# Convolution inputs and two gates of a hybrid layer as one run of Strassen pairs, with the gates and the residual kept in DRAM

## The chip, the core and the metric

The kernel runs on one core of a Trainium2 chip. The metric is the device time of one execution in microseconds (us). Five engines work side by side, each through its own list of instructions in order: TensorE (PE) multiplies, VectorE (DVE) and ScalarE (ACT) do elementwise work, GpSimd (POOL) does some of it and issues DMAs that add to what lies in SBUF, and SyncE (SP) issues the other DMAs. PE has two clock levels, 2.4 and 1.2 GHz; the profile gives the granted share of full speed.

## The reference

The input is a sequence of 512 positions with 1024 features (float32). Two hybrid layers run one after the other, then a second block that the change does not touch. One hybrid layer, cut to what matters here:

```python
def hybrid_layer(x, positions, ...):
    h = rmsnorm(x, norm_mix)
    proj = h @ w_in
    cb, cc, cu, q, k, v, g, ga, gb = jnp.split(proj, split_points, axis=-1)
    y_conv = short_conv_mixer(cb, cc, cu, conv_w, w_conv_out)   # (cb * conv3(cc * cu)) @ w_conv_out
    y_ret = retention_mixer(q, k, v, g, positions, ret_norm, w_ret_out)
    merged = jax.nn.sigmoid(ga) * y_conv + jax.nn.sigmoid(gb) * y_ret
    x = x + merged @ w_o
    h2 = rmsnorm(x, norm_mlp)
    return x + jnp.square(jax.nn.relu(h2 @ w_up)) @ w_down
```

The convolution inputs cb, cc, cu and the gates ga, gb are 1024 columns each, so five of the products here are 1024 x 1024.

## The kernel before

Activations lie transposed: a tile has 128 features on the partitions and 512 positions, and x is 8 such tiles. To keep float32 accuracy every operand is split into a high and a low part, and each block product is three matmuls (`mm3`, L282 to L284: high x whi, low x whi, high x wlo).

**Weights** come in units of up to eight 128 x 128 blocks, in the order in which PE uses them. SP loads a unit into one of seven raw buffers (`load_to`, L203), so the load of unit u+7 waits until unit u is split. ACT makes the high part (`whi`, L232) and DVE the low part (`wlo`, L233) in `part_to`. Strassen units also need sums of weight blocks: POOL issues a DMA that adds a second stretch of DRAM to the raw buffer (`sum_to`, L214, tile `wa`), and DVE adds one raw unit onto another (L229). `advance` asks for loads 9 units ahead, sums 7 ahead and splits 2 ahead.

**Products.** `dense` makes one 128 x 512 output tile from 8 block products, that is 24 matmuls of 512 columns. `strassen` makes pairs of output tiles with seven half-width products per block pair: 7 x 4 x 3 = 84 matmuls of 256 columns in place of 48 of 512 columns. It takes its operands from seven "factors" of each pair of input tiles, which `halves` makes. Before, only w_up uses it, in four quarters of four pairs. Product f of pair j is written (f, j); PE takes them in an order written out by hand.

**Order of a layer.** In `b1_layer`: the convolution inputs by `dense` for m = 0 to 7 (columns 1024 `ev_c`, 2048 `ev_u`, 0 `ev_b` of w_in); gate ga; w_conv_out (`ev_co`); four retention heads; gate gb; the gate g; w_ret_out (`ev_ro`); w_o; then the MLP. The norm of x is not waited for: its factor `rbc` is multiplied in when a product is taken out of PSUM, and the sum of squares, its reduction by PE (L516) and the broadcast (L528) run beside the first products. Small pieces of work (the norm chain, the rotary tables, retention pieces) lie in a list `bg`; `pulse` takes one off when PE has been given 4.5 us of products (`due`) since the last.

## Time and profile before

| | |
|---|---|
| time, median of 3 runs | 2538.9 us (2536.22 to 2543.73) |
| the profiled execution | 2541.95 us |
| its span in the profile | 2540.2 us |
| PE busy | 2505.2 us (99%), 13150 matmuls |
| DVE, ACT, POOL busy | 1538.8 (61%), 1013.8 (40%), 355.8 (14%) us |
| mean granted PE clock | 0.993 of full |

The span is the stretch that the profile covers; the time has 1.75 us more around it. The profiled execution lies 3.05 us (0.12%) above the median of the three runs.

### The profile page before, as it was taken

The numbers are of one execution on the slowest core, as the hardware profiler recorded it, in microseconds if no ns is written. First come the engines' busy times: TensorE is split into PE (matmuls) and PEld (weight loads), VectorE is DVE, ScalarE is ACT, GpSimd is POOL, SyncE is SP. The second block draws the span as 40 slices with busy tenths as digits, with TensorE's granted clock in tenths as the row PEclk, the third lists the DMA queues.
The fourth block names the chain that finished last, engine by engine and source line by source line (L and its number), as shares of the span: only waits on it lengthen the run. The fifth ranks groups of instructions, "written<-read, shape, count | busy, mean of one in ns | idle before, by whom it ended". The sixth has DMA issues, their size and how long they took to land. (4 is left out here: it accounts for less than half of the span.)

```text
span 2540.2 us, 33110 instructions
## 1 busy us (share of the span) xinstructions
PE 2505.2 (99%) x13150; PEld 2139.2 (84%) x13150; DVE 1538.8 (61%) x2254; ACT 1013.8 (40%) x1672; POOL 355.8 (14%) x338
## 2 busy tenths in 40 slices
PE   8999999999999999999999999999999999999998
PEld 7888988888899888889887998898867888888886
DVE  6544655575666654356467665676679565673773
ACT  4222434353453422234335553354586444322221
POOL 2100110220001211011012101013100111220111
PEclk9999999999999999999999999999999999999999
DMA  5333222265666332322223665563301322233221
GB/s 201 108 98 98 78 75 84 89 176 159 169 191 176 119 100 98 99 86 79 80 96 93 195 190 151 161 187 104 107 27 34 100 92 83 91 100 100 91 95 46
DMA packets 87692, 286.22 MB, mean 113 GB/s; under 512 B 9904, under 2 KB 9904, under 8 KB 87408
## 3 DMA queue, kind: packets, MB, share of 16 engines
q1 hardware_dynamic: 76032, 256.56, 30.5%
q0 software_dynamic: 10784, 26.48, 6.2%
q8 instruction: 103, 1.69, 0.3%
q10 hardware_dynamic: 720, 1.05, 0.1%
q14 instruction: 53, 0.43, 0.1%
HBM read 281.96 MB, written 2.10 MB: 112 GB/s over the span
## 5 line engine op out<-in xcount | busy, mean ns | idle before, releaser
L282 PE MATMUL mm<-hi,whi 128*128 128x512 f32 x2528 | 989.7, 391 | 6.2 <-ACT hi L274 6.2
L284 PE MATMUL mm<-hi,wlo 128*128 128x512 f32 x2528 | 986.3, 390 | 0.1
L283 PE MATMUL mm<-lo,whi 128*128 128x512 f32 x2528 | 985.5, 390 | 0.5 <-DVE lo L277 0.5
L233 DVE TENSOR_TENSOR wlo<-raw,whi 128x1024 fp32r<-128x1024 f32 (+2 forms) x512 | 608.4, 1194 | 288.3 <-ACT whi L232 285.9
L232 ACT ACTIVATE whi<-raw 128x1024 fp32r<-128x1024 f32 (+2 forms) x512 | 502.2, 995 | 373.6 <-PE mm L283 312.3
L284 PEld LDWEIGHTS mm<-hi,wlo 128*128 128x128 f32 x2528 | 475.4, 188 | 103.3 <-DVE wlo L233 3.6
L282 PEld LDWEIGHTS mm<-hi,whi 128*128 128x128 f32 x2528 | 475.9, 188 | 102.6 <-ACT hi L274 6.2
L283 PEld LDWEIGHTS mm<-lo,whi 128*128 128x128 f32 x2528 | 475.8, 188 | 97.8 <-DVE lo L277 1.0
L539 POOL TENSOR_TENSOR ssq<-ssq,sq 128x512 f32<-128x512 f32 x65 | 91.4, 1406 | 537.1 <-ACT sq L274 528.0
L282 PE MATMUL sa<-tf,whi 128*128 128x256 f32 x512 | 147.1, 287 | 5.3 <-ACT y L274 5.3
L284 PE MATMUL sa<-tf,wlo 128*128 128x256 f32 x512 | 147.0, 287 | 1.1 <-DVE wlo L233 1.1
L283 PE MATMUL sa<-tf,whi 128*128 128x256 f32 x512 | 146.1, 285 | 0.0
L214 POOL DMA_DIRECT2D raw<-wa x72 | 62.2, 864 | 504.0 <-DMA raw<-ws 229.1
L769 DVE TENSOR_TENSOR dn<-mm,rbc 128x512 f32<-128x512 f32 x64 | 44.2, 690 | 126.2 <-PE mm L284 126.1
L282 PEld LDWEIGHTS sa<-tf,whi 128*128 128x128 f32 x512 | 99.1, 194 | 6.4 <-ACT y L274 5.7
L284 PE MATMUL sb<-tf,wlo 128*128 128x256 f32 x352 | 99.8, 283 | 1.9 <-DVE wlo L233 1.9
L284 PEld LDWEIGHTS sa<-tf,wlo 128*128 128x128 f32 x512 | 99.2, 194 | 2.6 <-DVE wlo L233 2.5
L283 PE MATMUL sb<-tf,whi 128*128 128x256 f32 x352 | 99.8, 283 | 0.9 <-DVE tf L277 0.9
L282 PE MATMUL sb<-tf,whi 128*128 128x256 f32 x352 | 100.0, 284 | 0.0
L283 PEld LDWEIGHTS sa<-tf,whi 128*128 128x128 f32 x512 | 99.3, 194 | 0.3
L881 PE MATMUL nat<-whi,hi 128*128 128x256 f32 (+2 forms) x320 | 94.9, 297 | 0.0
L882 PE MATMUL nat<-wlo,hi 128*128 128x256 f32 (+2 forms) x320 | 94.2, 294 | 0.0
(361 smaller groups left out, 3170.6 us busy)
## 6 DMA issues: line engine op xcount, KB each, us to landing
raw<-ws SPq DMA_DIRECT2D x444, 512.0 KB, 3.4
raw<-ws SPq DMA_DIRECT2D x64, 256.0 KB, 3.3
raw<-wa POOLq DMA_DIRECT2D x48, 256.0 KB, 5.2
raw<-wa POOLq DMA_DIRECT2D x24, 512.0 KB, 5.5
x<-x SPq DMA_DIRECT2D x8, 256.0 KB, 5.8
raw<-ws SPq DMA_DIRECT2D x4, 384.0 KB, 3.0
dec<-dec SPq DMA_DIRECT2D x1, 1024.0 KB, 10.0
mem<-mem POOLq DMA_DIRECT2D x4, 256.0 KB, 4.9
```

The costliest lines, as they stand in the source:

```text
L214: self.nc.gpsimd.dma_start(self.raw[u][:, at:at + n], self.d["wa"][self.more_at[u]][:, :n], accum_op=ALU.add)
L232: self.nc.scalar.activation(hi[:, :n], w, AF.Copy)
L233: tt(lo[:, :n], w, hi[:, :n].bitcast(F32), op=ALU.subtract)
L282: mm(out, w[0], x[0], start=start, stop=False, **kw)
L283: mm(out, w[0], x[1], start=False, stop=False, **kw)
L284: mm(out, w[1], x[0], start=False, stop=stop, **kw)
L539: self.nc.gpsimd.tensor_tensor(st["ssq"], st["ssq"], q, op=ALU.add)
L769: tt(t, p, self.rbc2, op=ALU.mult)
L881: mm(p, xc[0], w[0][:, :n], start=k == 0, stop=False)
L882: mm(p, xc[0], w[1][:, :n], start=False, stop=False)
```

## The change

In each hybrid layer the convolution inputs of m = 2 to 7 (9 pairs) and both gates (8 pairs) become one run of 17 Strassen pairs; m = 0 and 1 stay dense. The run's factors are made by the new `factors` from x and the split tiles that exist already: four pairs of input tiles, each with nine DVE operations of up to 256 columns and five ACT operations. They stand in `bg` behind the norm chain and the rotary tables, and whatever is still in `bg` after the two dense groups is put out at once, before the first pair. The gates (as sigmoids), the gated convolution m1 and the residual x no longer wait in SBUF: `away` writes each tile of 256 KB to DRAM on ACT's queue, and `back` reads it on SP's queue, ga in `ev_co`, and gb, m1 and x in `ev_ro`. Two additions or products go from POOL to DVE, one scaling from DVE to ACT. The retention heads take background work every 3 us. The first quarter of w_up starts with five products without their last input pair (`early`). The core of the diff:

```diff
+    def away(self, x, what):
+        t = self.dp.tile([P, S], F32, tag=what, name=self.name(what), bufs=KD)
+        self.nc.scalar.dma_start(t, x)
+        return t
+    def back(self, t, what):
+        x = self.slot(what=what)
+        self.nc.sync.dma_start(x, t)
+        return x
...
-            for v in [v for v in w if v < u - 1 and v != self.cur]:
+            for v in [v for v in w if v < min(u - 1, self.pinned) and v != self.cur]:
...
+    def factors(self, xs, k, x1, x2, g1, g2):
+        tt = self.nc.vector.tensor_tensor
+        st, out = {}, {}
+        for f, (m, e) in {1: (k, 0), 2: (k + 1, 0), 3: (k + 1, 1)}.items():
+            out[f] = [t[:, e * H:(e + 1) * H] for t in xs[m]]
+        def split(f, v):
+            t = self.slot(S, True, "tf")
+            out[f] = t[:, :H], t[:, H:]
+            self.act(t[:, :H], v)
+            self.lo(t[:, H:], v, t[:, :H])
+        def first():
+            y, t, n = self.slot(what="ty"), self.slot(what="tu"), self.sm(1, "ng")
+            st["y"], st["t"] = y, t
+            self.nc.vector.tensor_scalar(n, g2, -1.0, None, op0=ALU.mult)
+            self.act(y, x1, AF.Copy, scale=g1)
+            tt(t[:, H:], y[:, :H], y[:, H:], op=ALU.subtract)
+            self.stt(t[:, :H], x2[:, H:], n, y[:, H:])
+            split(5, t[:, H:])
+        def second():
+            y, t, u = st.pop("y"), st.pop("t"), self.slot(what="tv")
+            tt(u[:, :H], t[:, :H], y[:, :H], op=ALU.subtract)
+            self.stt(u[:, H:], x2[:, :H], g2, u[:, :H])
+            for f, v in ((7, t[:, :H]), (6, u[:, :H]), (4, u[:, H:])):
+                split(f, v)
+        return out, [first, second]
...
+        if early:
+            open_pair(1)
+            y0 = unit([(6, 0)], x0)
+            self.pinned = at[1, 0][0]
+            first = [(1, 0), (2, 0), (7, 0), (1, 1), (2, 1)]
+            for x in first:
+                product(*x, ks=range(K - 1), split=1)
+            for f, j in first:
+                product(f, j, ks=[K - 1], split=1)
+                if f == 1:
+                    keep(j, 1)
+                elif f == 2 and j == 0:
+                    self.pinned = x0
+                    self.part_to(y0 + 1)
+                elif f == 7:
+                    self.pinned = MOST
+                    self.part_to(y0 + 2)
...
+        X = []
+        for k in range(0, KD, 2):
+            def begin(k=k):
+                out, steps = self.factors(xs, k, self.x[k], self.x[k + 1], *[self.prm(f"mix{i}", m) for m in (k, k + 1)])
+                X.append(out)
+                self.bg[:0] = steps
+            self.bg.append(begin)
...
-            nc.vector.tensor_scalar(y, z[:, 2:], self.prm(f"conv{i}_2", m), None, op0=ALU.mult)
+            self.act(y, z[:, 2:], AF.Copy, scale=self.prm(f"conv{i}_2", m))
...
-            t, y = self.slot(what="b"), tmp["y"]
-            tt(t, p, self.rbc, op=ALU.mult)
-            nc.gpsimd.tensor_tensor(t, t, y, op=ALU.mult)
-            bz[m] = yield from self.split_late(t)
-        for m in range(KD):
+            y = tmp.pop(("y", m))
+            tt(y, y, self.rbc, op=ALU.mult)
+            tt(y, p, y, op=ALU.mult)
+            bz[m] = yield from self.split_late(y)
+        for m in range(2):
...
-        m1 = [None] * KD
-        def ev_gate(m, p):
-            t = self.slot(what="gate")
-            tt(t, p, self.rbc, op=ALU.mult)
-            self.act(t, t, AF.Sigmoid)
-            m1[m] = t
-        self.dense(xs, [c8(W, 6144, m) for m in range(KD)], ev_gate)
+        while self.bg:
+            self.tick(0.0)
+        for m in range(KD):
+            self.x[m] = self.later[m]
...
+        def gate(what):
+            def ev(m, y):
+                tt(y, y, self.rbc, op=ALU.mult)
+                yield
+                self.act(y, y, AF.Sigmoid)
+                away[what, m] = self.away(y, what)
+            return ev
...
+        evs, pairs = [], []
+        for m in range(2, KD, 2):
+            for o, ev in ((1024, ev_c), (2048, ev_u), (0, ev_b)):
+                evs.append((ev, m))
+                pairs.append([c8(W, o, m), c8(W, o, m + 1)])
...
+        for o, what in ((6144, "ga"), (7168, "gb")):
+            for m in range(0, KD, 2):
+                evs.append((gate(what), m))
+                pairs.append([c8(W, o, m), c8(W, o, m + 1)])
...
+        self.strassen(X, pairs, done)
...
+            t = self.back(away.pop(("ga", m)), "ga")
+            tt(t, p, t, op=ALU.mult)
+            yield
+            away["m1", m] = self.away(t, "m1")
...
+        self.due = 3.0
...
-        sgb = [None] * KD
-        def ev_sgb(m, p):
-            t = self.slot(what="sgb")
-            tt(t, p, self.rbc, op=ALU.mult)
-            self.act(t, t, AF.Sigmoid)
-            sgb[m] = t
-        self.dense(xs, [c8(W, 7168, m) for m in range(KD)], ev_sgb)
...
-            t = self.slot(what="mg")
-            tt(t, p, sgb[m], op=ALU.mult)
-            nc.gpsimd.tensor_tensor(t, t, m1[m], op=ALU.add)
+            t, m1 = self.back(away.pop(("gb", m)), "gb"), self.back(away.pop(("m1", m)), "m1")
+            tt(t, p, t, op=ALU.mult)
+            tt(t, t, m1, op=ALU.add)
+            del m1
+            self.x[m] = self.back(x[m], "x")
...
-            self.strassen(xm, [[c8(f"w_up{i}", (quarter * Q + 2 * j + e) * P, 0) for e in range(2)] for j in range(Q // 2)], up)
+            self.strassen(xm, [[c8(f"w_up{i}", (quarter * Q + 2 * j + e) * P, 0) for e in range(2)] for j in range(Q // 2)], up, quarter == 0)
...
+        if later:
+            self.later[m] = self.away(x, "x")
...
-        self.bg += [scores((0, 1)), scores((2, 3)), lambda: None, outs, var, scale]
+        gap = lambda: None
+        self.bg += [scores((0, 1)), scores((2, 3)), gap, gap, outs, var, scale]
```

What this does to the order on the engines is shown at three places; names end in the buffer number of each program, which is not the same in both.

**POOL at the start of the program.** `ssq` collects the squares of x (`sq`), `rstd` is the norm's factor, `raw7` the eighth unit of weights. Before:

```order
L1787 UNCONDITIONAL_BRANCH [waits barrier_Pool_Activation_PE_DVE_SP_gather]
L539 ISA
L539 TENSOR_TENSOR ssq_30_191<-ssq_30_191,sq_31_193 128x512 [waits Activation_49]
...
L539 TENSOR_TENSOR ssq_30_191<-ssq_30_191,sq_37_241 128x512 [waits Activation_49,Pool_49]
L521 TENSOR_TENSOR rstd_40_282<-ms_39_280,mhalf_100 128x4 [waits DVE_49]
```

and now:

```order
L1906 UNCONDITIONAL_BRANCH [waits barrier_Pool_Activation_PE_DVE_SP_gather]
L226 DMA raw7_161<-wa 128x512 [waits DMAHW4_49,DMAHW1_49,DVE_49]
L624 ISA
L624 TENSOR_TENSOR ssq_30_194<-ssq_30_194,sq_31_196 128x512 [waits Activation_49]
...
L624 TENSOR_TENSOR ssq_30_194<-ssq_30_194,sq_37_244 128x512 [waits Activation_49,Pool_49]
L606 TENSOR_TENSOR rstd_40_285<-ms_39_283,mhalf_102 128x4 [waits DVE_49]
```

The adding DMA of unit 7 stands ahead of the seven additions, and it waits for the load of raw7.

**DVE in the first layer, behind the last product of m = 1** (`b` and `y` are taken from PSUM there, L662 and L755). `turns` and `rest` are the rotary tables' range reduction, `ng`, `tu`, `tv` and `tf` belong to the factors, `wlo8` is the low part of the ninth unit. Before:

```order
L662 TENSOR_TENSOR b_57_414<-mm_56_382,rbc_43_320 128x512
L588 TENSOR_SCALAR turns_60_419<-ang_55_379 128x512
...
L596 TENSOR_SCALAR rest_61_420<-rest_61_420 128x512
L233 TENSOR_TENSOR wlo8_442<-raw8_161,whi8_441 128x1024
L647 TENSOR_TENSOR c_63_461<-mm_62_429,rbc2_44_322 128x512
```

and now:

```order
L755 TENSOR_TENSOR y_53_379<-mm_55_386,y_53_379 128x512
L673 TENSOR_SCALAR turns_58_423<-ang_54_383 128x512
...
L681 TENSOR_SCALAR rest_61_435<-rest_61_435 128x512
L299 TENSOR_TENSOR lo_57_422<-y_53_379,hi_56_421 128x512
L712 TENSOR_TENSOR trig_10_107<-trig_10_107,rbc_43_324 128x512
L713 TENSOR_TENSOR trig_10_107<-trig_10_107,rbc_43_324 128x512
L417 TENSOR_SCALAR ng_64_450<-par_71 128x1
...
L299 TENSOR_TENSOR tf_91_527<-tu_87_515,tf_91_527 128x256
L299 TENSOR_TENSOR tf_93_533<-tv_90_524,tf_93_533 128x256
L245 TENSOR_TENSOR wlo8_543<-raw8_163,whi8_542 128x512
```

Before, one table's reduction (8 operations) lies between this product and wlo8; now both tables' reductions (15), a split, the tables' two products with rbc and the 36 operations of the factors do. `tf_91` is factor 7 of the last input pair, which product (7, 0) takes. In the second layer the same stretch holds three and a half input pairs and no rotary reductions.

**SP beside w_ret_out in the first layer.** The loads of weights (`raw`) and, now, the tiles read back. Before:

```order
L203 DMA raw84_3605<-ws 128x1024
L203 DMA raw85_3644<-ws 128x1024
L203 DMA raw86_3682<-ws 128x1024
L203 DMA raw87_3720<-ws 128x1024
L203 DMA raw88_3758<-ws 128x1024
```

and now, behind nine tiles for m = 0 to 2:

```order
L215 DMA raw120_4784<-ws 128x1024
L192 DMA gb_508_4817<-gb_203_2630 128x512
L192 DMA m1_509_4819<-m1_221_2949 128x512
L192 DMA x_510_4823<-x 128x512
L215 DMA raw121_4828<-ws 128x1024
L192 DMA gb_514_4862<-gb_204_2719 128x512
L192 DMA m1_515_4864<-m1_224_2985 128x512
L192 DMA x_516_4868<-x 128x512
L215 DMA raw122_4873<-ws 128x1024
```

Three reads stand behind each load, and a load waits until the unit seven before it is split. On DVE the product and the sum with gb_508 and m1_509 (L834, L835) stand ahead of wlo114, the unit for which raw121 waits.

## Rows read from the trace of the kernel before

**Rows 1.** The page, busy time, share of the span, instructions.

```profile
PE 2505.2 (99%) x13150; PEld 2139.2 (84%) x13150; DVE 1538.8 (61%) x2254; ACT 1013.8 (40%) x1672; POOL 355.8 (14%) x338
```

**Rows 2.** Timeline of PE in dense products: start, us, engine, line.

```profile
45.01 0.39 PE L282 MATMUL mm<-hi,whi 128*128 128x512 f32 x1
...
55.21 0.39 PE L282 MATMUL mm<-hi,whi 128*128 128x512 f32 x1
```

**Rows 3.** Stretches: length, busy (instructions) by engine, PE clock, DMA share, GB/s.

```profile
5.00:27.00 22.00, 18.50 (x72) 14.52 (x72) 14.11 (x14) 15.05 (x22) 10.40 (x7) 1.00 1.03 404
617.80:658.50 40.70, 40.70 (x337) 40.43 (x336) 29.44 (x41) 24.00 (x42) 5.12 (x6) 1.00 0.81 217
```

**Rows 4.** DVE's groups in 617.8 to 658.5 (a w_up quarter): busy, mean ns.

```profile
L233 DVE TENSOR_TENSOR wlo<-raw,whi 128x1024 fp32r<-128x1024 f32 (+1 forms) x17 | 16.9, 1002 | 5.7 <-ACT whi L232 5.6
L229 DVE TENSOR_TENSOR raw<-raw,raw 128x1024 f32<-128x1024 f32 (+1 forms) x4 | 4.4, 1088 | 3.7 <-DMA raw<-wa 3.7
L487 DVE TENSOR_TENSOR y<-sb,y 128x256 f32<-128x256 f32 x4 | 1.7, 421 | 1.6 <-ACT y L274 1.5
```

**Rows 5.** Timeline of SP, POOL and PE at the start, idle before and its releaser.

```profile
14.34 0.33 SPq L203 DMA_DIRECT2D raw<-ws  x1
...
16.13 11.19 POOL L539 TENSOR_TENSOR ssq<-ssq,sq 128x512 f32<-128x512 f32 x7 [15.68 <-ACT sq L274]
...
27.38 1.86 PE L516 MATMUL ssq<-ones,ssq 128*128 128x1 f32 x8 [2.21 <-POOL ssq L539]
...
37.06 0.60 PE L528 MATMUL bc<-con,rstd 128*128 128x128 f32 x4
```

**Rows 6.** DMA issues, KB, us to landing: 14.2 to 14.9 us, then the page.

```profile
raw<-ws SPq DMA_DIRECT2D x1, 512.0 KB, 11.1
...
raw<-ws SPq DMA_DIRECT2D x444, 512.0 KB, 3.4
raw<-ws SPq DMA_DIRECT2D x64, 256.0 KB, 3.3
```

**Rows 7.** The page's group of the adding DMA's issue on POOL.

```profile
L214 POOL DMA_DIRECT2D raw<-wa x72 | 62.2, 864 | 504.0 <-DMA raw<-ws 229.1
```

**Rows 8.** Timeline of DVE in the first layer.

```profile
50.92 0.68 DVE L662 TENSOR_TENSOR b<-mm,rbc 128x512 f32<-128x512 f32 x1
...
58.57 0.42 DVE L588 TENSOR_SCALAR turns<-ang 128x512 f32<-128x512 f32 x1
...
62.13 0.43 DVE L596 TENSOR_SCALAR rest<-rest 128x512 f32<-128x512 f32 x1
...
68.73 0.68 DVE L627 TENSOR_TENSOR trig<-trig,rbc 128x512 f32<-128x512 f32 x1
```

**Rows 9.** Timeline of DVE: nine operations of `halves`, first and last.

```profile
518.48 0.14 DVE L409 TENSOR_SCALAR ng<-par 128x1 f32<-128x1 f32 x1
...
521.37 0.42 DVE L287 TENSOR_TENSOR tf<-tv,tf 128x256 fp32r<-128x256 f32 x1
```

**Rows 10.** Timeline of DVE in the second layer, products u and b of m = 1.

```profile
901.25 0.69 DVE L653 TENSOR_TENSOR z<-mm,c 128x512 f32<-128x512 f32 x1 [2.22 <-PE mm L284]
...
906.69 0.69 DVE L662 TENSOR_TENSOR b<-mm,rbc 128x512 f32<-128x512 f32 x1 [1.45 <-PE mm L284]
```

**Rows 11.** Timeline of DVE in w_ret_out of the first layer.

```profile
457.63 1.23 DVE L233 TENSOR_TENSOR wlo<-raw,whi 128x1024 fp32r<-128x1024 f32 x1 [1.66 <-ACT whi L232]
...
460.72 0.69 DVE L720 TENSOR_TENSOR mg<-mm,sgb 128x512 f32<-128x512 f32 x1 [0.65 <-PE mm L284]
...
482.48 0.69 DVE L720 TENSOR_TENSOR mg<-mm,sgb 128x512 f32<-128x512 f32 x1 [1.92 <-PE mm L284]
```

**Rows 12.** Timeline of PE in the first quarter of w_up.

```profile
534.83 0.39 PE L282 MATMUL sa<-tf,whi 128*128 128x256 f32 x1 [2.64 <-ACT y L274]
...
536.02 0.41 PE L282 MATMUL sa<-tf,whi 128*128 128x256 f32 x1
...
539.23 0.36 PE L282 MATMUL sb<-tf,whi 128*128 128x256 f32 x1
```

More of the change, by code (lines that the diff above doesn't have):

```diff
@@ L398, in halves @@
             for f, v in ((1, y[:, :H]), (5, t[:, H:])):
-                out[f] = self.slot(S, True, "tf")
-                self.act(out[f][:, :H], v)
-                self.lo(out[f][:, H:], v, out[f][:, :H])
+                out[f] = new()
+                self.act(out[f][0], v)
+                self.lo(out[f][1], v, out[f][0])
             return
@@ new lines, in open_pair, with keep, seven @@
+        def open_pair(j):
+            A[j], B[j] = self.ps("sa"), self.ps("sb")
+            Y[j] = self.slot(what="y1"), self.slot(what="y2")
+            unit([(1, j), (2, j)])
+        def keep(j, f):
+            e, h = {1: (0, 0), 6: (1, 0), 5: (1, 1), 3: (0, 1)}[f]
+            self.act(Y[j][e][:, h * H:(h + 1) * H], A[j][:, :H], AF.Copy, scale=-1.0 if f == 6 else 1.0)
+        def seven(j):
+            tt(Y[j][1][:, H:], B[j][:, H:], Y[j][1][:, H:], op=ALU.subtract)
+            tt(Y[j][0][:, :H], B[j][:, :H], Y[j][0][:, :H], op=ALU.add)
@@ new lines, in strassen @@
+        open_pair(0)
+        x0 = unit([(7, 0)])
+        if early:
[15 more added lines that the diff above has]
+                    self.part_to(y0 + 2)
+        else:
+            unit([(6, 0)], x0)
+            product(1, 0)
+            keep(0, 1)
+            product(2, 0)
+            product(7, 0)
@@ new lines, in strassen @@
+        product(6, 0)
+        keep(0, 6)
+        for j in range(n):
+            new = j + 1 if j + 1 < n else None
+            if new is not None and new not in A:
+                open_pair(new)
+            xu = unit([(7, new), (5, j)])
+            if new is None:
+                unit([(4, j)])
+            unit([(6, new), (3, j)], xu)
+            if new is not None:
+                unit([(4, j)])
+                if j or not early:
+                    product(1, new)
+                    keep(new, 1)
+                    product(2, new)
+                    product(5, j)
+                    keep(j, 5)
+                    product(7, new)
+                else:
+                    product(7, new)
+                    product(5, j)
+                    keep(j, 5)
+                seven(j)
+                product(6, new)
+                keep(new, 6)
+                product(3, j)
+                keep(j, 3)
+                product(4, j)
+                tt(Y[j][1][:, :H], B[j][:, H:], Y[j][1][:, :H], op=ALU.add)
+            else:
+                product(5, j)
+                keep(j, 5)
+                seven(j)
+                E[j] = self.ps("se")
+                product(4, j)
+                tt(Y[j][1][:, :H], B[j][:, H:], Y[j][1][:, :H], op=ALU.add)
+                tt(Y[j][1][:, :H], E[j][:, :H], Y[j][1][:, :H], op=ALU.add)
+                product(3, j)
+                keep(j, 3)
+            y1, y2 = Y.pop(j)
+            del A[j], B[j]
+            E.pop(j, None)
+            self.active += self.step(done(j, y1, y2))
@@ L1685, in program @@
         self.setup()
-        self.st, self.xs = {}, []
+        self.st, self.xs, self.later = {}, [], [self.d["x"][k] for k in range(KD)]
         for k in range(KD):
```

100 lines of the change are left out of this document (35 added, 65 removed).

## The prediction

> **What bounds the kernel now.** I read the page's busy times first. PE is busy for 2505 of 2540 us [rows 1]: the time is the number of matmul columns, and everything else matters only where it makes PE wait. Then the timelines, for what a column costs. Between two starts in dense work lie 45 matmuls of 512 columns in 10.20 us, 0.227 us each [rows 2]. In a w_up quarter, 337 matmuls of 256 columns start in 40.70 us, 0.121 each [rows 3]. A pair of output tiles thus takes PE 48 x 0.227 = 10.88 us dense and 84 x 0.121 = 10.14 us by Strassen.
>
> The same quarter shows the price: DVE is busy for 29.44 of 40.70 us, and the DMA engines at 0.81 with 217 GB/s [rows 3]. DVE's weight work and the combinations out of PSUM are 16.9 + 4.4 us and eleven operations of 0.42 us [rows 4], 25.9 us or 6.5 us a pair. So a Strassen pair has little room on either.
>
> **The change, part by part.**
>
> *The pairs.* There are 17 per layer, 34 in all. At the quarter's rate they save 34 x 0.74 = 25.2 us, the most that the change can give on PE. A convolution triple (c, u, b) adds 14 operations of 512 columns on DVE (two, six and six), some 0.68 us each [rows 8], 9.5 us. With 3 x 6.5 that is 29.0 us of DVE in 30.4 of PE, and u and b alone (10.6 each) are over 10.14. I take 10.4 us for these 18 pairs, which saves 8.6. A gate pair writes two tiles of 256 KB, 0.52 MB, on top of 217 GB/s x 10.18 us = 2.21 MB, which takes the DMA share from 0.81 to 1.00. I take 10.6 for these 16, which saves 4.5. Together **-13**. Bounds: -25, and +14 if the pairs take 11.3.
>
> *POOL at the start.* PE waits 2.21 us for POOL's seven additions, which run from 16.13 to 27.32 [rows 5]. Now the adding DMA of unit 7 stands ahead of them and waits for raw7. That load is issued at 14.34 [rows 5] and takes 11.1 us in the crowd of the start [rows 6], so to 25.4; it is half as large now, which at 404 GB/s [rows 3] is 0.6 us less: 24.8. Issuing the addition takes POOL 0.86 us [rows 7]. The additions then begin at 25.7; they took 11.19 us, I take 10.2 since DVE is quieter then. They end at 35.9 instead of 27.3, and the norm's factor, on which all evictions wait, moves by as much: **+8.6** (7 to 10).
>
> *The burst of background work, first layer.* The broadcast is on PE at 37.06 [rows 5]; 0.4 us for it and 48 matmuls behind it end dense m = 1 at 48.4. Unstalled, the first four half products (4 x 12 x 0.121 = 5.8) would end at 54.2. But DVE takes the last dense product only at 50.92 [rows 8], at 53.0 with the change's own operations (two products of 0.6 with rbc and the sum onto raw8 more, two scalings of 0.5 less, short waits for ACT). Behind it stand the rotary reductions: the second table's took from 58.57 to 62.56, 4.0 us [rows 8], the first has one more operation, 4.4, so to 61.4. A split and two table products of 0.6 us: 63.3. Then 36 factor operations; nine of the same sizes took 518.48 to 521.79, 3.3 us [rows 9], so 13.2: 76.5. Only then comes wlo8, for product (6, 0), and factor 7 of the last input pair is hardly earlier. PE can do (1, 0), (2, 0) and most of (7, 0) meanwhile, and ends (6, 0) at 78.4. Stall: **+24.2** (20 to 28), on top of the shift at the start.
>
> *The burst, second layer.* No reductions, and DVE keeps up: it waits 1.45 us for PE before it takes b of m = 1 at 906.69 [rows 10]. The first half of the first input pair fits into that wait and the 2.22 us before it. Then b's two operations to 907.6, five factor operations 2.0, a split 0.6, three input pairs 9.9, the half wlo 0.6: 920.7, and (6, 0) ends at 922.0 instead of 906.6 + 5.8 = 912.4. **+9.6** (7 to 13).
>
> *Reading back.* No row shows these reads, so they are bounded. A load of 512 KB lands in 3.4 us, one of 256 KB in 3.3 beside others [rows 6]; at 404 GB/s [rows 3] the bytes of the first are 1.3 us, so some 2.1 are fixed. In w_ret_out, a load and three reads (1.31 MB) take 2.1 + 3.2 = 5.3, without the x tile 4.7; I take 5.0. DVE then needs 1.2 for product and sum and 1.2 for the next wlo, which frees the next load on SP: with 0.3 of handing over, a step of 7.7 us, where PE takes 5.44. The first step starts with the wlo that ends at 458.86 [rows 11], so the merge of m = 3 is at 463.9 instead of 460.72, and that of m = 7 at 463.9 + 4 x 7.7 = 494.7 instead of 482.48 [rows 11]. The low part of m = 6 stands behind that merge on DVE: 496.5. PE has six of eight inputs of two w_o products to do first, 36 x 0.227 = 8.2 after 482.4, and waits from 490.6: 5.9, taken as 5.5 since the first reads are early. Two layers: **+11** (4 with a step of 7.0, 20 with 8.7). In w_conv_out one tile is read: 2.1 + 1.9 + 0.6 + 1.2 + 0.2 = 6.0 against 5.44, seven times 0.56 less a lead of 2: **+4** in two layers (0 to 8).
>
> The start's row shows 404 GB/s [rows 3]. The Trainium skill, "DMA: Bandwidth & Descriptors", section "Where 436 GB/s comes from", says that about 358 GB/s of HBM binds such transfers; by that the read step would be an estimated 0.8 us longer and w_o's wait 4 us per layer, 8 in all. The row is above that limit, so the sum goes by the row.
>
> *PE's clock.* After an idle of 2.64 us, 15 matmuls from 536.02 to 539.23 ran at 0.214 us, the lower level, 1.4 us lost [rows 12]. Two long new stalls, taken as 2 each: **+4** (3 to 8).
>
> *The early start* of w_up aims at that wait, 2.64 + 1.4 per layer. But the second pair's products need a unit whose low part stands on DVE behind the last input pair's nine operations, so I take 1.5 per layer: **-3** (0 to -8).
>
> POOL's products that go to DVE are in the counts above; ACT at 40% hides the scaling, the factors' ACT work fits beside DVE's, and writes on ACT's queue cost issue only.
>
> **Sum.** 8.6 + 24.2 + 9.6 - 13 + 11 + 4 + 4 - 3 = +45.4 on the profiled 2541.95 gives 2587.3; that execution is 3.05 above the median, so 2584.3 on the scale of the runs shown: **2584 us**, 1.8% slower. About 0.3% is what a measurement of this kernel can tell from no change.
>
> **The rivals.**
>
> *DVE is faster than I count (other side).* If the bursts hide, the pairs run at 10.14 and the read step falls to 6.5 us so that its waits go, what stays is 8.6 - 25.2 - 3 = -19.6: 2519 us. It decides in the runs' favour once start, bursts, read-backs and clock cost less than 25.2 + 3 - 7.6 = 20.6 together, against 61 above. For it: DVE idles for 28% of a quarter. Against: the burst is one list in order, and PE's fourth product is at its end. Chance 0.05.
>
> *The Strassen run stalls in pieces.* If each convolution triple leaves DVE behind, PE waits as in w_up's start, 2.64 us and 1.4 at the lower clock [rows 12]; six triples, +24: 2608 us. For it: 29.0 of 30.4 us of DVE; against: u and b overlap with c's slack. Chance 0.15.
> The row shows one such drop after one wait. The Trainium skill, "TensorE: Matmul & The Clock Gate", section "HAM oscillation — how this bites in real kernels", tells of a loop of short matmul groups with waits between, in which the clock falls again at every wait; this rival is that, on a small scale, and the quarters' full clock [rows 3] speaks against it.
>
> *The reads hide.* If backs are issued far enough ahead, the 11 and 4 go: 2569 us. For it: the first nine stand ahead of the first waiting load. Chance 0.15.
>
> **How the numbers follow.** My forecast has 0.65, with 2566 to 2604 of its own. The range 2556 to 2616 takes in the last two rivals and the bounds of pairs and bursts; some 0.2 is outside. Faster 0.05 (the first rival), same 0.04 (its half-way), slower 0.91.
>
> **What would show it.** In the profile after: PE idle before `ssq` of some 10 us; two waits of PE behind dense m = 1, some 24 and 10 us in all, released by DVE's `tf` or wlo; pairs of 10.4 to 10.6 us at full clock; PE waits at w_o's seventh input, released by a split behind `gb`. It is wrong if the bursts are under 20 us together, or if the pairs take less than 10.2 or more than 11 us.

## The result and the profile after

The changed kernel takes **2620.85 us** (median of 4 runs, 2616.31 to 2624.03), the kernel before 2537.89 beside it: ratio **1.0323** (95% interval 1.0309 to 1.0338). It is 83 us slower; 2584 was forecast, and 2620.85 lies above the range. The spans of the two profiled executions are 2540.2 and 2617.1 us, 76.9 apart, and the sums below are made on these (the profiled execution before lies 3.05 us above its median, the one after 1.9 below).

The page, busy time by engine, answers to [rows 1]:

```profile
PE 2510.4 (96%) x14374; PEld 2192.9 (84%) x14374; DVE 1692.3 (65%) x2554; ACT 1141.3 (44%) x1936; POOL 352.2 (13%) x376
```

PE's share fell from 99% to 96%: it is busy for 5 us more and idle for 72 more. What it waits for, in the view of waits (engine, operation and line, what ended the wait, us in all, times, longest):

```profile
PE sb L294 <- ACT tf L286: 21.4, 7, 13.0
PE sa L294 <- ACT y L286: 14.5, 9, 3.2
PE ssq L601 <- POOL ssq L624: 10.2, 1, 10.2
PE sa L296 <- DVE wlo L245: 10.1, 10, 1.8
PE sa L294 <- ACT whi L244: 6.5, 2, 3.6
PE mm L294 <- ACT hi L286: 6.1, 1, 6.1
PE mm L295 <- DVE lo L299: 5.5, 3, 3.0
PE sb L295 <- DVE tf L299: 4.6, 7, 0.7
```

The wait for `hi` was there before, behind other work. The first, third and eighth are the two bursts and the start, as forecast; the seventh is w_o behind the tiles read back. The second, fourth and fifth were not in the sum as waits.

The timeline of PE and POOL from the start to the bursts (start, us, engine, line, operation, in brackets the idle time before it and what ended it) answers to [rows 5]:

```profile
25.77 1.06 POOL L226 DMA_DIRECT2D raw<-wa  x1 [25.32 <-DMA raw<-ws]
26.63 9.63 POOL L624 TENSOR_TENSOR ssq<-ssq,sq 128x512 f32<-128x512 f32 x7
...
36.32 1.01 PE L601 MATMUL ssq<-ones,ssq 128*128 128x1 f32 x4 [10.24 <-POOL ssq L624]
...
73.25 0.58 PE L294 MATMUL sb<-tf,whi 128*128 128x256 f32 x1 [12.96 <-ACT tf L286]
...
83.23 0.58 PE L294 MATMUL sb<-tf,whi 128*128 128x256 f32 x1 [1.23 <-ACT tf L286]
...
961.48 0.58 PE L294 MATMUL sb<-tf,whi 128*128 128x256 f32 x1 [2.10 <-ACT tf L286]
```

The adding DMA stands first on POOL and ends its wait at 25.77 (forecast 24.8); `ssq` comes to PE at 36.32 (forecast 35.9, before 27.38). In the opening of the run PE waits once for 12.96 us and then 1.2 to 1.4 us for each input pair's factors in turn.

Stretches of the run in the first layer (length, busy time and instructions of PE, PEld, DVE, ACT, POOL, PE clock, DMA share, GB/s) answer to [rows 3]. The first is the opening with its 48 matmuls, the next five hold 84 matmuls each: a clean one, two with the work of a u pair, a clean one between, and the third u pair's:

```profile
57.26:88.15 30.89, 11.30 (x50) 8.74 (x48) 29.09 (x65) 14.99 (x28) 0.84 (x1) 0.60 0.20 50
99.36:109.44 10.08, 10.08 (x86) 10.08 (x85) 7.61 (x10) 4.90 (x9) 1.25 (x2) 1.00 0.91 258
109.44:121.35 11.91, 10.33 (x87) 10.13 (x86) 10.00 (x14) 6.13 (x11) 1.84 (x4) 1.00 0.78 188
141.51:157.11 15.60, 12.07 (x86) 11.66 (x85) 11.57 (x15) 6.10 (x11) 2.77 (x6) 0.89 0.77 210
167.19:177.27 10.08, 10.08 (x86) 10.08 (x85) 8.65 (x12) 4.90 (x9) 0.89 (x2) 1.00 0.93 245
177.27:191.30 14.03, 11.83 (x86) 11.62 (x85) 10.44 (x14) 6.12 (x12) 2.93 (x6) 0.88 0.81 210
```

A pair that is not disturbed takes 10.08 us. What is over that I call the excess: in the first layer 11.3 us for the three u pairs and 7.4 for the eight gate pairs, in the second 10.4 and 7.2. (The expectations below, written over 10.04 us a pair, have 0.1 to 0.2 more.) ACT is busy for 6.1 of 15.60 us in the worst stretch. That stretch more closely, in the timeline of ACT, DVE and PE (`z` and the `y` made from it belong to the convolution, `y<-sa` takes a product out of PSUM, L241 adds one raw unit of weights onto another):

```profile
142.71 1.23 DVE L241 TENSOR_TENSOR raw<-raw,raw 128x1024 f32<-128x1024 f32 x1 [3.65 <-issue]
...
145.32 0.68 DVE L745 TENSOR_TENSOR z<-y,c 128x512 f32<-128x512 f32 x1
...
146.03 0.72 ACT L286 ACTIVATE y<-z,par 128x512 f32<-128x512 f32 x1 [4.44 <-DVE z L745]
...
146.86 1.54 DVE L289 SCALAR_TENSOR_TENSOR y<-z,par,y 128x512 f32<-128x512 f32 x2 [0.86 <-ACT y L286]
...
148.31 1.22 DVE L245 TENSOR_TENSOR wlo<-raw,whi 128x1024 fp32r<-128x1024 f32 x1
149.45 0.69 DVE L745 TENSOR_TENSOR z<-y,c 128x512 f32<-128x512 f32 x1
150.17 0.72 ACT L286 ACTIVATE y<-z,par 128x512 f32<-128x512 f32 x1 [2.46 <-DVE z L745]
150.80 0.36 ACT L286 ACTIVATE y<-sa 128x256 f32<-128x256 f32 x1
...
151.22 0.39 PE L294 MATMUL sa<-tf,whi 128*128 128x256 f32 x1 [3.20 <-ACT y L286]
...
152.34 0.42 PE L296 MATMUL sa<-tf,wlo 128*128 128x256 f32 x1
152.55 0.42 PE L294 MATMUL sa<-tf,whi 128*128 128x256 f32 x1
```

The product to be taken out is the first of this stretch, 12 matmuls from 141.51 on and so complete at some 143.1, but ACT takes it out at 150.80, and PE needs its bank again: the second scaling stands ahead of that copy and waits for DVE's second `z`, which stands behind a low part, two accumulations, and 0.86 us of waiting for the first scaling. The first `z` is late as well: DVE stood still for 3.65 us before the sum at 142.71, which stands ahead of it, and what ended that wait the profile does not show. ACT idles 4.44 and 2.46 us meanwhile. Behind the gap matmuls start 0.21 us apart at 152.34, the lower clock.

In w_ret_out SP and DVE work in a ring (the timeline again; `gb` is the gate read back):

```profile
503.53 0.33 SPq L215 DMA_DIRECT2D raw<-ws  x1
503.95 0.38 SPq L192 DMA_DIRECT2D gb<-gb  x1
...
507.84 0.69 DVE L834 TENSOR_TENSOR gb<-mm,gb 128x512 f32<-128x512 f32 x1 [4.34 <-DMA gb<-gb]
...
509.24 1.22 DVE L245 TENSOR_TENSOR wlo<-raw,whi 128x1024 fp32r<-128x1024 f32 x1
...
510.48 0.33 SPq L215 DMA_DIRECT2D raw<-ws  x1
```

One step, from load to load, is 6.95 us (forecast 7.7, and PE takes 5.44).

**Where the 76.9 us are**, from the starts of PE's matmuls in both traces:

| | forecast | measured |
|---|---|---|
| start to the end of dense m = 1 | +8.6 | +8.9 |
| openings of the run, with their clock | +24.2 + 9.6 + 4 | +25.1 + 11.4 + 1.9 |
| the pairs of the run | -13 | **+9.0** |
| w_conv_out to w_o (read back) | +11 + 4 | +7.8 + 9.7 |
| first w_up quarter (early start) | -3 | **+6.0** |
| other w_up quarters | 0 | -2.9 |

The 216.27 and 201.17 us of the run are 47.5 over 34 dense pairs of 10.88; less the openings' 38.5 that leaves the 9.0.

### The profile page after: what moved, and what is told of

Its sections match the earlier page's. It is cut to its first block, busy times and chain, and to the rows that moved or that the text cites. A ratio compares the mean times of both kernels' runs of the same rounds, so it can differ in the third digit from the quotient of the medians.

```text
span 2617.1 us, 36753 instructions
## 1 busy us (share of the span) xinstructions
PE 2510.4 (96%) x14374; PEld 2192.9 (84%) x14374; DVE 1692.3 (65%) x2554; ACT 1141.3 (44%) x1936; POOL 352.2 (13%) x376
## 5 line engine op out<-in xcount | busy, mean ns | idle before, releaser
L245 DVE TENSOR_TENSOR wlo<-raw,whi 128x1024 fp32r<-128x1024 f32 (+1 forms) x584 | 667.5, 1148 | 301.8 <-ACT whi L244 299.6
L294 PE MATMUL mm<-hi,whi 128*128 128x512 f32 x1984 | 779.5, 393 | 6.1 <-ACT hi L286 6.1
L295 PE MATMUL mm<-lo,whi 128*128 128x512 f32 x1984 | 775.5, 391 | 6.0 <-DVE lo L299 5.5
L296 PE MATMUL mm<-hi,wlo 128*128 128x512 f32 x1984 | 776.5, 391 | 0.8 <-DVE wlo L245 0.6
L244 ACT ACTIVATE whi<-raw 128x1024 fp32r<-128x1024 f32 (+1 forms) x584 | 558.7, 971 | 346.2 <-PE mm L295 209.0
L295 PEld LDWEIGHTS mm<-lo,whi 128*128 128x128 f32 x1984 | 374.2, 189 | 83.9 <-DVE lo L299 7.1
L294 PE MATMUL sa<-tf,whi 128*128 128x256 f32 x784 | 226.8, 289 | 21.0 <-ACT y L286 14.2
L296 PE MATMUL sa<-tf,wlo 128*128 128x256 f32 x784 | 226.6, 289 | 10.1 <-DVE wlo L245 10.1
L295 PE MATMUL sa<-tf,whi 128*128 128x256 f32 x784 | 225.0, 287 | 0.0
L294 PE MATMUL sb<-tf,whi 128*128 128x256 f32 x616 | 178.3, 289 | 23.3 <-ACT tf L286 21.4
L295 PE MATMUL sb<-tf,whi 128*128 128x256 f32 x616 | 177.9, 289 | 4.6 <-DVE tf L299 4.6
L294 PEld LDWEIGHTS sa<-tf,whi 128*128 128x128 f32 x784 | 153.2, 195 | 24.0 <-ACT y L286 16.6
L295 PEld LDWEIGHTS sa<-tf,whi 128*128 128x128 f32 x784 | 153.6, 196 | 0.3
L294 PEld LDWEIGHTS sb<-tf,whi 128*128 128x128 f32 x616 | 120.7, 196 | 25.6 <-ACT tf L286 23.3
L295 PEld LDWEIGHTS sb<-tf,whi 128*128 128x128 f32 x616 | 120.4, 196 | 6.8 <-DVE tf L299 6.7
```

What stands on the lines that cost most here:

```text
L244: self.nc.scalar.activation(hi[:, :n], w, AF.Copy)
L245: tt(lo[:, :n], w, hi[:, :n].bitcast(F32), op=ALU.subtract)
L294: mm(out, w[0], x[0], start=start, stop=False, **kw)
L295: mm(out, w[0], x[1], start=False, stop=False, **kw)
L296: mm(out, w[1], x[0], start=False, stop=stop, **kw)
```

## The experiments

The theory after the two traces: each stall of the run is an order on an in-order engine. Beside the forecast openings these are ACT's scaling ahead of the copies out of PSUM, POOL's zeros, and the gates' writes taking DMA time from the weights. The rivals: the later waits are a tail of the burst, or DVE has simply too much to do, or it waits for late sums of weights. Each edit is on the changed kernel, and medians stand against its 2620.85; the kernel before took 2535.97 to 2537.66 beside them.

**The openings.** `e1_ga_dense` makes gate ga by dense products ahead of the run, as cover for the burst, and leaves 13 pairs:

```diff
+        def ev_ga(m, p):
+            t = self.slot(what="y")
+            tt(t, p, self.rbc, op=ALU.mult)
+            yield
+            self.act(t, t, AF.Sigmoid)
+            away["ga", m] = self.away(t, "ga")
+        self.due = 2.0
+        self.dense(xs, [c8(W, 6144, m) for m in range(KD)], ev_ga)
+        self.due = 4.5
...
-        for o, what in ((6144, "ga"), (7168, "gb")):
+        for o, what in ((7168, "gb"),):
```

> Gate ga stays dense and stands between the two dense convolution groups and the Strassen run (13 pairs per layer instead of 17), and background work is taken every 2 us there, so the rotary tables and the factors come out beside eight dense products. My theory, that the stalls are a matter of the order on DVE and POOL: the waits of PE for factors at the run's start (26 and 12 us) and 8 of the 10 us before the sum of squares go, eight pairs cost 0.8 us more each, so 8.9 + 38 - 6.5 = 40 us less than the changed kernel's 2621: about 2581. Rival, that DVE has no room for this work anywhere: it only comes back as other waits of PE in ga, and no more than the 9 at the start is gained: 2612 or above.

Measured 2566.76 us, 1.0113 (1.0093 to 1.0134), 14 below the theory's 2581. Both openings take 5.75 us, no excess at all, and the waits for `tf` are gone from the list, which now begins:

```profile
PE sa L294 <- ACT y L286: 10.5, 6, 2.6
PE sa L294 <- ACT whi L244: 7.3, 2, 3.6
...
PE ssq L601 <- POOL ssq L624: 1.9, 1, 1.9
```

The start's wait fell too, from 10.2 to 1.9, since unit 7 is a dense one there and nothing is added to it. The u pairs still lose 1.8 to 2.9 each.

`e5_free_factors`:

```diff
-        return out, [first, second]
+        out.update({5: out[1], 7: out[2], 6: out[3], 4: out[3]})
+        return out, []
```

> The changed kernel without the operations of the new factors: products 4 to 7 of a pair take tiles that exist already, so 36 DVE and 20 ACT operations per layer are left out and the output is another; pairs, weights, gates and reads are the same. In the second layer the burst is gone, in the first the rotary tables' 10 us are left. My theory now: the waits inside the later pairs (19 and 18 us beyond 10.04 us a pair) are the tail of the burst, since DVE has 29.0 of 30.2 us to do in a triple and cannot catch up with the weight units that it left: in the second layer the opening's excess falls from 11.4 to under 1 and that of the later pairs from 18 to some 6, the first layer loses its 25 down to some 11 and some of its 19: 40 to 50 us less, 2570 to 2580. Rival: the later waits belong to the pairs themselves (scaling on ACT, late sums of weights): they stay at 18 and 19, and only the openings fall: 25 us less, 2595.

Measured 2594.96 us, 1.0224 (1.0201 to 1.0247). The opening loses nothing in the second layer and 11.9 in the first, one wait of 10.02 us: that much is the rotary reductions, and the factors are the rest. But the later pairs' excess did not fall, 18.9 us in the second layer where 17.6 stood. My own theory of a tail of the burst falls with that.

**The start.** `e4_pool` asks for the first sums later, so that the adding DMA stands behind `ssq` on POOL:

```diff
-        self.sum_to(u + ACCUMULATE)
+        self.sum_to(u + ACCUMULATE if u > 2 else 6)
```

> Only the first sums of weights are asked for later, so that unit 7's adding DMA stands behind POOL's seven additions. My theory: PE's wait before the sum of squares is 2.2 instead of 10.2 us and everything behind moves up, 8 to 9 us less: 2612. Rival: unit 7, now summed later, is late for the fourth product, or the time is lost again in the burst on DVE: less than 3 us, 2618 to 2621.

Measured 2610.19 us, 1.0292 (1.0272 to 1.0312), 10.7 less. Dense m = 1 ends at 44.77 instead of 57.26, and the opening's excess stays 25.1. That is also 3.6 us earlier than in the kernel before (48.41): PE waits 0.83 us for `ssq` there instead of 2.21 [rows 5], and from 20 to 40 us the granted clock stays at 1.00, where it was 0.87 and 0.79.

**The u pairs.** `e2_scale_dve` takes the scaling back to DVE:

```diff
-            self.act(y, z[:, 2:], AF.Copy, scale=self.prm(f"conv{i}_2", m))
+            nc.vector.tensor_scalar(y, z[:, 2:], self.prm(f"conv{i}_2", m), None, op0=ALU.mult)
```

> Only the first scaling of the convolution goes back from ACT to DVE. My theory: on ACT it waits for DVE's product z, and what stands behind it on ACT, the copy that empties the PSUM bank of the pair before, waits with it, and PE for that bank (up to 3.4 us in each u pair). With the scaling on DVE that copy goes ahead: the run's waits beyond the first pair, 19 and 18 us, fall by at least half, 15 to 20 us less: 2601 to 2606. Rival: DVE is the limit of these pairs (29.0 of 30.2 us in a triple), and 12 operations of 0.5 us more on it make the run longer: 2621 to 2627.

Measured 2612.59 us, 1.0304 (1.0285 to 1.0323), 8 less. PE's waits:

```profile
PE sa L296 <- DVE wlo L245: 15.8, 14, 3.0
...
PE sb L294 <- DVE y L520: 6.3, 6, 1.1
...
PE sa L294 <- ACT y L286: 1.3, 2, 0.7
```

The wait for ACT went from 14.5 to 1.3, but DVE's own lateness took much of it: low parts from 10.1 to 15.8, and 6.3 for DVE's part of the products. The u pairs' excess fell from 21.7 to 16.3 us in both layers. Half right.

`e8_zeros_dve` has DVE write the two zero columns ahead of each `z`:

```diff
-            nc.gpsimd.memset(z[:, 0:2], 0.0)
+            nc.vector.memset(z[:, 0:2], 0.0)
```

> Only the two columns of zeros ahead of the convolution's z are set by DVE instead of POOL. My theory, since the last runs did not bear out that the later waits are the burst's tail: on POOL those zeros stand behind the adding DMAs of later units, which wait for loads, and DVE's next step of the convolution waits for the zeros (2.5 us in one u pair), ACT's copies for DVE and PE for the bank. What is left in a u pair is then the 1.9 us of the scaling on ACT: the conv pairs' excess falls from 11.4 and 10.5 us to some 6 per layer, 10 us less: 2611. Rival: the sums of weights themselves are late there, and DVE waits for them instead: 2618 or above.

Measured 2615.64 us, 1.0306 (1.0291 to 1.032), 5 less (10.5 by the spans), where 10 were expected. The three u pairs of the first layer fell from 1.8, 5.5 and 4.0 to 1.8 each, those of the second from 1.8, 2.5 and 6.0 to 1.8, 1.8 and 4.3. In the changed kernel two zeros stand behind adding DMAs on POOL, and DVE's accumulations wait for them, as here in its timeline:

```profile
180.04 0.85 POOL L226 DMA_DIRECT2D raw<-wa  x1 [0.37 <-issue]
...
180.58 0.46 POOL L744 MEMSET z<- 128x2 f32 x2
181.04 1.54 DVE L289 SCALAR_TENSOR_TENSOR y<-z,par,y 128x512 f32<-128x512 f32 x2 [1.49 <-POOL z L744]
```

The zeros are not the whole of it, and the rival of late sums holds for some pairs. In the one that lost 5.5 us DVE waited for no zeros, but for 3.65 us before the sum at 142.71; the pair that still loses 4.3 us here has such a wait too, and with the zeros on DVE in c7 below u pairs lose up to 6.2 us behind waits of over 3 us. In this kernel and in c7:

```profile
1051.03 1.23 DVE L241 TENSOR_TENSOR raw<-raw,raw 128x1024 f32<-128x1024 f32 x1 [2.02 <-issue]
```

```profile
115.52 1.23 DVE L241 TENSOR_TENSOR raw<-raw,raw 128x1024 f32<-128x1024 f32 x1 [3.63 <-DMA raw<-wa]
```

In c7's row an adding DMA ends the wait. No run takes this wait away alone.

`e11_late_scale` leaves the scaling on ACT, but one product later for each of the two tiles, with the accumulations:

```diff
+        def conv(m):
+            z, y = tmp.pop(("z", m)), self.slot(what="y")
...
                 if e == 0:
                     yield
+            if ev is ev_u:
+                for e in range(2):
+                    yield
+                    conv(m + e)
```

> The changed kernel, where the scaling of a u pair stays on ACT but each of the two (with its two accumulations on DVE) is given one product later, behind ACT's first copy out of PSUM instead of ahead of it. Theory (the scaling stands ahead of the copies on ACT and waits for z, and PE waits for the bank): in the u pairs of both layers, which lose 11.4 and 10.5 us now, the first 1.9 of each goes, -11 in all, about 2609 us; what DVE owes for its zeros on POOL stays. Rival (DVE is late with its own work there, as in the run with the scaling on DVE): the waits move to a low part and the time stays within 3 us of 2621.

Measured 2611.77 us, 1.0294 (1.0274 to 1.0313), 9 less, between the two theories. The stretch of 15.60 us takes 10.40, and the next one 11.49 instead of 10.08 (stretches as above):

```profile
139.73:150.13 10.40, 10.33 (x87) 10.13 (x86) 9.34 (x14) 5.75 (x11) 1.84 (x4) 1.00 0.90 234
150.13:161.62 11.49, 10.59 (x87) 10.18 (x85) 8.90 (x13) 5.81 (x11) 1.93 (x3) 1.00 0.98 275
```

PE's wait for ACT's copies fell from 14.5 to 2.2 us, none longer than 0.8; that for low parts went from 10.1 to 17.7. The convolution pairs lose 4 us in the first layer and 8 in the second, where it was 11.3 and 10.4 in the u pairs, while the gate pairs lose 4 more in all. So the order on ACT made about half of these stalls, and behind it lies a smaller one of DVE and the weights.

**DMA traffic.** `e9_no_gate_dma`:

```diff
-                away[what, m] = self.away(y, what)
...
-            t = self.back(away.pop(("ga", m)), "ga")
-            tt(t, p, t, op=ALU.mult)
+            t = self.slot(what="ga")
+            tt(t, p, self.rbc, op=ALU.mult)
...
-            t, m1 = self.back(away.pop(("gb", m)), "gb"), self.back(away.pop(("m1", m)), "m1")
-            tt(t, p, t, op=ALU.mult)
+            t, m1 = self.slot(what="gb"), self.back(away.pop(("m1", m)), "m1")
+            tt(t, p, self.rbc, op=ALU.mult)
```

> The gates are computed as before but neither written to DRAM nor read back: the norm's factor is multiplied in their place, so the output is another. My theory: writing them fills the DMA engines beside the weight loads (share 1.02 in one stretch of gate pairs), the weights' lead shrinks pair by pair, and PE waits for weight units in the second half of the gates: their excess falls from 7.5 and 7.4 us to under 3 per layer; with two thirds of the reads left, w_conv_out and w_ret_out give back some 3 more per layer: 14 to 16 us less, 2606. Rival: these waits come from the adding DMAs alone, and only the reads' 6 us go: 2615.

Measured 2591.76 us, 1.0215 (1.0202 to 1.0229), 29 less, twice what was expected. The gate pairs' excess falls from 7.4 and 7.2 to 2.2 and 1.4, 11 us in all, as the theory has it. The rest is mostly the reads, of which half are gone (32 of 64): w_conv_out to w_o takes 293.7 us in both layers instead of 300.2 and 302.1, 15 us where 6 were expected. The gates' stretch, of the changed kernel and then of this one:

```profile
202.00:273.00 71.00, 66.04 (x533) 64.15 (x532) 48.43 (x68) 39.78 (x66) 9.36 (x11) 1.00 0.95 271
```

```profile
200.00:270.00 70.00, 68.46 (x557) 67.51 (x556) 52.78 (x74) 41.07 (x69) 10.24 (x12) 1.00 0.88 244
```

`e6_backs_act` issues the reads on ACT's queue:

```diff
-        self.nc.sync.dma_start(x, t)
+        self.nc.scalar.dma_start(x, t)
```

> Only the reads back from DRAM are issued on ACT's queue instead of SP's. My theory: the waits at the end of w_ret_out and in w_o (PE for DVE's low parts, 5.5 us) come from reads and weight loads standing in one list on SP, each load behind a split and each split behind a read; with two lists they fall under 2 us: 4 to 8 us less, 2613 to 2617. Rival: a read on ACT waits for its buffer in front of ACT's own splits, and those hold up PE as long: 2619 or more.

Measured 2601.91 us, 1.025 (1.0226 to 1.0273), 19 less and more than the theory's 4 to 8; w_conv_out to w_o takes 294.0 us in both layers, which is 14 of it, and PE's waits in w_o are gone. What DVE's operations on `gb` waited for, in the changed kernel and here (us, times):

```profile
  DMA gb<-gb: 44.2, 15
```

```profile
  DMA gb<-gb: 4.9, 4
```

The reads lag no more once they do not stand behind weight loads that wait for a free buffer; the bytes are the same.

**The early start.** `e3_no_early`:

```diff
-            self.strassen(xm, [[c8(f"w_up{i}", (quarter * Q + 2 * j + e) * P, 0) for e in range(2)] for j in range(Q // 2)], up, quarter == 0)
+            self.strassen(xm, [[c8(f"w_up{i}", (quarter * Q + 2 * j + e) * P, 0) for e in range(2)] for j in range(Q // 2)], up)
```

> Only the early start of the first w_up quarter is left away. My theory: the first quarter took 3.3 and 2.8 us longer than before because the five early products split only one unit ahead, so PE meets four weight units just being split; without it both are back: 6 us less, 2615. Rival: the longer quarter comes from what the reading back of x leaves on DVE and SP, and stays: 2621 or, as the early start was a gain, 2624.

Measured 2610.69 us, 1.0295 (1.0275 to 1.0315), 10 less (8.4 by the spans), where the first quarters alone give 4.4 (50.0 and 47.6 us instead of 51.4 and 50.6). The other 4 of the spans lie ahead of these quarters, in stretches that the edit leaves as they are. In the changed kernel PE waits there for splits of weights:

```profile
577.14 0.38 PE L294 MATMUL sb<-tf,whi 128*128 128x256 f32 x1 [1.11 <-ACT whi L244]
578.85 0.58 PE L296 MATMUL sb<-tf,wlo 128*128 128x256 f32 x1 [1.20 <-DVE wlo L245]
583.59 0.58 PE L294 MATMUL sa<-tf,whi 128*128 128x256 f32 x1 [2.88 <-ACT whi L244]
```

**Several at once.** `e10_four_fixes` is e4, e8, e6 and e3 together.

> The changed kernel with four single edits of these runs together: the adding DMA of unit 7 behind POOL's additions, the zeros by DVE, reads issued on ACT, no early start. All 17 pairs per layer and the burst stay. My theory, that these are separate waits: their gains add up, 9 + 8 + 13 + 7 = 37 us less than 2621: 2584, and what is left over the kernel before is the burst (38 us) and the last waits in the pairs. Rival: behind the burst the same wait only changes its name, and less than 25 us are gained: 2596 or above.

Measured 2582.9 us, 1.0181 (1.0166 to 1.0197), 38 less. The four alone are 10.7, 5.2, 18.9 and 10.2 by their medians, 45.0: the pieces are mostly separate. It is still 46 us above the kernel before, and its two runs are the place: 215.4 and 200.1 us, where 17 dense pairs take 185.0 each.

The others start from e1, so that the opening is covered. c1 adds e2, e8 and e3; c7 adds e8, e6 and e3; c8 is c7 with the later scaling of e11.

> The gate ga dense and ahead of the run (as in the first experiment), the first scaling of the convolution back on DVE, the two columns of zeros set by DVE instead of POOL, and no early start. My theory: from 2566.8 the six waits of a bank of 1.7 to 2.6 us shrink to about 1, 5 us less, and the first quarters 4 us less: 2557. Rival: with DVE fuller in the u pairs the waits move to its weight units: 2562 to 2567.

> As the first experiment (gate ga dense ahead of the run, 13 pairs per layer), with the zeros by DVE, reads on ACT and no early start; the scaling stays on ACT. My theory: from 2567 the reads give back 10 to 13 us, the early start 4 to 6, the zeros 1: 2548 to 2552, still above the kernel before by the heads' extra time (3 to 4 us per layer) and 1.9 us in each u pair. Rival: with the reads on ACT, ACT's list becomes the limit in w_conv_out: 2555 or above.

> Kernel c7 (gate ga dense ahead of the run, zeros by DVE, reads on ACT, no early start), with the same later scaling. Its u pairs still lose 12 and 11 us of 10.04 each. Theory: with zeros on DVE nothing but the scaling is left, so most of it goes: -16 us, about 2520 us and 0.994 of the kernel before. Rival (DVE's own work): 2535, as c7, with PE waiting for low parts.

c1 measured 2555.94 us, 1.007 (1.005 to 1.009), as forecast; c7 2536.51, 0.9998 (0.999 to 1.0007), 12 better than forecast; c8 2533.22, **0.9985** (0.9975 to 0.9996), which missed: 2520 was expected, and its rival had 2535. In c7 the u pairs lose 11.4 and 10.6 us over 10.08, in c8 the runs are 7.4 and 3.4 us shorter. Of the 16 expected that is two thirds, in the span (2536.8 to 2530.8) 6 are left, and by the medians 3.

c2, c4, c5, c6 and c9 make gate gb dense too and keep it in SBUF, which leaves nine pairs. c2 is otherwise c1; c4 has six of ga's eight products ahead of the run and two behind, and the reads on ACT, and c5 also the scaling on ACT; c6 is c2 with two of gb's products behind the run and the reads on ACT; c9 is c6 with the later scaling on ACT.

> As the kernel c1, and gate gb as well dense and where it stood before, behind the heads and kept in SBUF, with the heads' background work taken every 4.5 us: only nine convolution pairs per layer are left as Strassen. My theory: gb's products cover the heads' last work, so the 3.6 us per layer that the heads take more than before go, and gb is not read back; 18 pairs at 0.8 save 14 less some 7 of waits in u pairs, m1, ga and x still cost some 3 per layer: 2530 to 2538, so level with the kernel before or just under. Rival: the heads' extra time comes from the DMAs, and the loss stays at 10 per layer: 2545 to 2555.

> As the kernel c2 (nine convolution pairs as Strassen, both gates dense), with two of gate ga's eight products behind the run instead of ahead of it, background work every 1.5 us in the six ahead of it, and reads issued on ACT. My theory: in c2 w_conv_out waits 7.5 and 5.9 us for the low parts of the last convolution tiles, because it follows the last pair at once; two dense products of 5.4 us each cover that, so 12 us less than c2's 2544, 2528 to 2534, under the kernel before by 0.1 to 0.3%. Rival: the waits belong to the reads of ga in w_conv_out and stay: 2540 or above.

> As the kernel c4, with the convolution's first scaling on ACT as in the change. My theory: with DVE ahead of its work this costs what it did in the first experiment, 1.9 us a u pair, where c4 has 1.0 to 2.6 from DVE's own load: within 3 us of c4. Rival: ACT's wait for z holds up its weight splits too: 6 us or more above c4.

> As the kernel c2 (nine convolution pairs, both gates dense, all eight products of ga ahead of the run), with two of gate gb's eight products right behind the run and reads on ACT. My theory: ga's eight products are enough to hide the background work, which six in c4 were not, and two products of gb cover the last convolution tiles ahead of w_conv_out: 10 to 13 us less than c2's 2544, 2531 to 2535, under the kernel before by up to 0.2%. Rival: the stall moves to gb's first product, as in c4 with ga's: 2540 or above.

> Kernel c6 (both gates dense, the second partly behind the run, nine pairs left), with the scaling moved from DVE to ACT and given later. Its pairs lose 4.9 and 4.7 us. Theory: half of that goes, -5 us, about 2532. Rival (other waits are left): within 2 us of 2537.

| | median us | ratio (95%) |
|---|---|---|
| c2 | 2543.9 | 1.003 (1.0016 to 1.0044) |
| c4 | 2555.16 | 1.0073 (1.0061 to 1.0085) |
| c5 | 2553.97 | 1.0073 (1.006 to 1.0086) |
| c6 | 2537.22 | 1.0004 (0.9995 to 1.0013) |
| c9 | 2529.83 | **0.9972** (0.9962 to 0.9982) |

c2 missed and lies just under its rival's 2545; c6 missed by 2 us. c4 missed by 21: six dense products do not hide the burst, and the first layer's opening loses 8.2 us again, as it does in c5, which is within 3 us of c4 as forecast. c9 is the fastest of all, 7.8 us under the kernel before. Its page:

```profile
PE 2489.1 (99%) x13798; PEld 2154.9 (85%) x13798; DVE 1631.5 (65%) x2474; ACT 1096.5 (43%) x1840; POOL 326.9 (13%) x328
```

Its two runs of nine pairs take 92.6 and 93.6 us, 10.3 and 10.4 a pair, against 97.9 dense: 9.6 us of gain, the sort of pair that the forecast had.

## Why the prediction was wrong

**The step that failed is "The pairs".** It took 10.4 us for a convolution pair and 10.6 for a gate pair, -13 in all; they came out at 11.3 and 11.0, +9.0. That is 22 of the 32 us between the forecast sum (+45.4) and the spans (+76.9); the early start is 9 more. The step's own bound, +14 at 11.3 us a pair, held. The mean of 10.14 [rows 3] was right for PE alone: clean pairs run at 10.08. The forecast then summed DVE's work over a triple, found that it fits, and put ACT off in one sentence: "ACT at 40% hides the scaling". A busy share says nothing on order. The scaling waits for DVE's `z` and stands ahead of the copy that frees PE's bank, so ACT idles and PE stands still. Moving the scaling one product later took PE's wait for ACT from 14.5 to 2.2 us and half of the u pairs' excess. What makes a u pair lose more than the 1.8 us of the scaling is DVE being late: in some it waits for POOL's zeros, which a run took away, in others for a sum of weights, which the traces show and no run tested. The gates' writes are 11 of the 15 us of the gate pairs. Which of the writes' effects it is (the engines' share, or the place on ACT's queue) was not taken apart.

**The rival "stalls in pieces"**, at 2608 us and a chance of 0.15, was nearest. It had 24 us of stalls in all, where the u pairs lost 21.7 and the gate pairs 14.6. It had DVE late, which is part of it, and not ACT's queue nor the gates; that it was near owes something to luck.

Behind the wait of 3.20 us at 151.22 the granted clock fell, and the stretch has 0.89. The Trainium skill, "TensorE: Matmul & The Clock Gate", section "HAM oscillation — how this bites in real kernels", tells of a loop of short matmul groups, with waits that are mostly longer, in which the clock falls at every wait. Here it did so only behind some: behind 2.20 us at 185.40, but not behind 2.28 at 1034.18, and the u pair at 109.44 with its wait of 1.6 us ran at 1.00.

**The start** (+8.6, measured 8.9) and **the bursts** (+24.2 and +9.6, measured 25.1 and 11.4) were right, and so were their causes: with the adding DMA behind `ssq` the start's wait goes, without the factors the second opening goes and the first halves, and eight dense products hide both. The clock lost 1.9 us behind the openings, and more in the u pairs, which the 4 did not mean.

**Reading back** was near in its sum (15, measured 17.5) by luck, though its ring on SP was shown by the reads on another queue (294.0 us in both layers, 292.4 before). Its parts were not right: the step is 6.95 us and not 7.7, w_o takes 4.1 us a layer more and not 5.5, w_conv_out 0.4 and not 2, and 4.1 and 4.4 us are lost between w_conv_out and w_ret_out, in the heads and the gate g, which the forecast did not have. Some 3 of these go with the reads' queue; the chain through the heads was not followed further. The prediction's estimate of a read step that is 0.8 us longer at the lower rate comes to some 0.4 by its own 1.31 MB; the sum did not use it.

**The early start** was to fill a wait [rows 12] and gain 3; it cost 6.0. The step's own doubt was the cause: five products take units whose splits are not made yet. Taking it away gave 4.4 us in the quarters; the other 6 of its 10 by the median stay open.

Of the other quarters four run at 40.31 us and two at 40.7, in place of 40.3 to 41.4, a gain of 3 that no term had. The diff also changes the order of the first products of a quarter; no run tests whether that is why.

## What to carry to other kernels

To move work to an engine that is idle 60% of the time, look at what stands behind it in that engine's list: if it waits there for a late producer, everything behind it does too, and copies that free PSUM must come first. Put preparation under work that PE can do without it before asking whether the faster method pays: 34 Strassen pairs lost 83 us with the burst bare, 18 (c9) gained 8 with it covered and the queues put right. Reads back from DRAM belong on a queue where no load waits for a free buffer.

## What the runs showed of the hardware that was not expected

In the gates' stretch the DMA engines were busy for 0.95 at 271 GB/s, and at the start for 1.03 at 404 GB/s [rows 3]. The page's queues of the changed kernel (packets, MB, share of 16 engines; q1 is SP's, q0 that of the adding DMAs) point to a reason:

```profile
q1 hardware_dynamic: 95616, 300.09, 33.8%
q0 software_dynamic: 20864, 53.22, 12.0%
```

A megabyte of the adding DMAs takes 0.225% of the engines' span, one of SP's 0.113%: twice as much, so where they run a full share goes with fewer GB/s. The share alone does not tell when weights come late: the clean stretch at 167.19 ran at 0.93 without a wait. And two zero columns, 0.46 us of work for two tiles on POOL, held DVE for 1.49 us behind such a DMA's issue, in a pair whose excess is 4.0 us with them there and 1.8 without.
